# One core, a tuned layer kernel: the model axis of adaLN in three stretches instead of two, and half of the gate's work beside the output stage

## The chip, the cores and the metric

One core of one Trainium2 chip runs the kernel. The metric is the device time in microseconds, median of the runs shown. TensorE (PE) does the matmuls, VectorE (DVE) and ScalarE (ACT) the elementwise work, SyncE (SP) and ScalarE issue the transfers.

## The reference

One layer with adaLN: a normalised input, modulated by a shift and a scale, is projected; 8 differential attention heads (group A) and 8 retention heads (group B) use the projection; one output projection follows, and a gate.

```python
mod = silu(c) @ ada_w + ada_b                 # ada_w: 4096 x 12288
shift, scale, gate = split(mod, 3)
mod_c = silu(c_ctx) @ ada_w[:, :2*D] + ada_b[:2*D]
h  = rms_norm(x,   norm_w) * (1 + scale)   + shift     # 256 x 4096
hc = rms_norm(ctx, norm_w) * (1 + scale_c) + shift_c   # 256 x 4096
proj = h @ w_in                               # q, k, v and gate columns of 16 heads
pc   = hc @ w_in[:, k and v columns]
...                                           # attention, retention, per-head norm, silu
y = concat([o_d, o_r]) @ w_out                # 256 x 4096 @ 4096 x 4096
return x + gate * y
```

## The kernel before, in words

Every matmul of a projection is done three times in float32r: the weights are split into a high part `whi` (a cast on ScalarE, L390) and a rest `wlo` (a subtraction on VectorE, L391), and the activations into `hh` and `hl` (in the output stage `ohh` and `ohl`); L404 to L406 multiply high by high, high by rest, rest by high. The 4096 model rows are 32 k-tiles of 128. A **unit** is one load of two k-tiles of weights (`raw`, three buffers), two `whi` and two `wlo` (four buffers each, so two units' worth) and 24 matmuls for keys and values ("kv": four row tiles, latent and context) or 12 for queries and gate columns ("qg": two row tiles). A heads have 512 columns, B heads 384.

Since `h` needs adaLN's shift and scale of a k-tile before that k-tile can be multiplied, the work is staged:

- **Stage 1**: TensorE takes adaLN of k-tiles 0 to 19 (`pa` L264, then `pm` L280 for each chunk of 1 or 2 k-tiles), and between its steps the kv matmuls of heads A0 to A4 over the k-tiles that are ready (L555 to L557).
- **Stage 2**: the kv of the other 11 heads (`FIRST`: A5 to A7, B0 to B7) over k-tiles 0 to 19; the partial sums are stored to DRAM (`p_dram`). Beside them VectorE takes adaLN of k-tiles 20 to 31 in three chunks of 4 (`ada2_task`: 32 loads `ada2` of 512 KB and two multiply-adds `acc` for each, L327; at a chunk's end 32 small matmuls `pm` L335 on TensorE, and the modulation of the chunk's `h`).
- **Main loop**: for each head the kv over k-tiles 20 to 31 (partials loaded at L491, added at L499) and the qg over all 32; attention or retention of earlier heads, and the gate, run beside it, steps of them after each unit (`between`). The gate is 128 steps: a load `graw` of 512 KB and two multiply-adds `gacc` on VectorE (L937, the first L935), and after every 16 steps a small matmul and a store of one column block of 512. `gate_rate` steps follow each unit: 2 in kv units of A heads, 1 in those of B heads, 0 in qg units.
- **Output stage**: 8 column blocks of 512, 16 units of 12 matmuls each (`O0_0` to `O7_15`). When a block is done, its gate row `gt` and input `xr` are loaded and the result `ot` is formed on VectorE (L1045, L1046).

Gate loads, `gacc`, `acc`, partials, `gt`, `xr`, `ot` and `ostg` (a head's output on its way back from DRAM) share one pool `a4` of 9 buffers. The instructions of an engine run in the order that the scheduler has laid down, which follows the program's order but lets later ones pass one that waits for a buffer. One SP queue issues all loads of `raw`, `ada`, `graw` and of the partials, in its own order.

Of the kernel before, what the change touches and what calls it, by code (L numbers as in the profile page):

```python
# [10 lines left out]
F32 = mybir.dt.float32  # L11
# [7 lines left out]
P = 128  # L19
# [19 lines left out]
K1 = 20  # L39
CHUNKS = [1, 1] + [2] * 9  # L40
CHUNKS2 = [4, 4, 4]
LEAD = 0.3
NS = 5
ADAB = 6
# [37 lines left out]
def hybrid_kernel(es, tc, x, c, ctx, c_ctx, norm_w, ada_w, ada_b, w_in, q_norm_w, k_norm_w,  # L82
# [132 lines left out]
    c0s2 = [K1 + sum(CHUNKS2[:j]) for j in range(len(CHUNKS2) + 1)]  # L215
# [87 lines left out]
    def ada2_task():  # L303

        work = [(j, k) for j in range(len(CHUNKS2)) for k in range(KT)]
        ahead = []

        def load():
            if len(ahead) < len(work):
                j, k = work[len(ahead)]  # L310
                ahead.append(ada_load(c0s2[j], CHUNKS2[j], k, f"ada2_{j}_{k}")[0])

        for _ in range(ADAB - 1):
            load()
        yield
        for i, (j, k) in enumerate(work):
            w = ahead[i]
            cn = CHUNKS2[j]
            n = cn * P
            if k == 0:  # L320
                acc = [a4.tile([P, 2 * n], F32, name=f"acc{j}_{v}", tag="a4") for v in range(2)]
            for v in range(2):
                cv = cT[:, v, k:k + 1]
                if k == 0:
                    nc.vector.tensor_scalar(acc[v], w, cv, None, op0=ALU.mult)
                else:
                    nc.vector.scalar_tensor_tensor(acc[v], w, cv, acc[v], op0=ALU.mult, op1=ALU.add)  # L327
            load()
            if k == KT - 1:
                yield  # L330
                pm = aux_tile([P, cn, 4], f"pm2_{j}")
                for q in range(cn):
                    for s in range(2):
                        for v in range(2):
                            nc.tensor.matmul(pm[:, q, 2 * s + v:2 * s + v + 1],  # L335
                                             acc[v][:, s * n + q * P:s * n + (q + 1) * P], ones[:, 0:1],
                                             start=True, stop=True)
                modulate(c0s2[j], cn, pm)
            yield
# [141 lines left out]
    def head_units(hd, qg, ktseq, part=False, rest=False):  # L481
# [4 lines left out]
        bank = Bank(f"ps{hd.name}{'p' if part else ''}_{qg}", nrt)  # L486
# [118 lines left out]
    ada2 = ada2_task()  # L605
    next(ada2)
    n_units = len(FIRST) * K1 // 2
    n_steps = len(CHUNKS2) * (KT + 1)
    done = [0, 0]

    def between1(i):
        done[0] += 1
        while done[1] < n_steps and done[1] < done[0] / (n_units - 10) * n_steps:
            next(ada2, None)
            done[1] += 1

    for nm in FIRST:
        run_units(head_units(heads[nm], 0, pairs(0, K1), part=True), between1)
    for _ in ada2:
        pass  # L620
# [291 lines left out]
    gate_done = [False]  # L912

    def gate_task():
# [35 lines left out]
        gate_done[0] = True  # L950
# [18 lines left out]
    def gate_step():  # L969
        next(gate, None)  # L970
# [127 lines left out]
```

## Time and profile before

| what | value |
|---|---|
| time, median of 3 runs | 2552.03 us (2547.63 to 2555.55) |
| profiled execution | 2548.96 us, its span 2547.1 us |
| mean granted clock of TensorE | 0.993 |
| PE busy | 2496.5 us (98%) |
| DVE busy | 1718.8 us (67%) |
| ACT busy | 1000.9 us (39%) |
| stages: 1 / 2 / main loop A, B / output, us from the span's start | 50 to 442 / to 944 / 956 to 1648, to 2169 / to 2541 |

The span is what lies between the first and the last instruction. TensorE's busy time counts overlapping matmuls, so the pace is read from matmul starts: in the output stage one in 0.234 us at 512 columns, for B heads one in 0.174 us at 384 columns.

### The profile page before, as it was taken

How to read it: one execution, taken by the hardware profiler on the slowest of the kernel's cores; microseconds unless marked ns; L12 is line 12 of the kernel's file. 1: busy time of each engine (PE TensorE's matmuls, PEld its weight loads, DVE VectorE, ACT ScalarE, POOL GpSimd, SP SyncE). 2: the span in 40 equal slices, each digit the busy share in tenths (PEclk: the TensorE clock that was granted, in tenths of full speed). 3: DMA queues.
4: the chain of work that ended last, by engine and by line, in shares of the span. 5: the costliest groups of instructions: out<-in, count | busy, mean ns of one | idle time of the engine just before them, and what ended most of it. 6: DMA issues, size and time to landing. Idle time of an engine off the chain costs nothing.

```text
span 2547.1 us, 36352 instructions
## 1 busy us (share of the span) xinstructions
PE 2496.5 (98%) x12634; PEld 2125.9 (83%) x12634; DVE 1718.8 (67%) x3028; ACT 1000.9 (39%) x2011; POOL 46.3 (2%) x49
## 2 busy tenths in 40 slices
PE   7899999999999999999999999999999999999999
PEld 4566667888999997788888888899999999788887
DVE  5555556965979546777877887777777666655554
ACT  5222222222323233354445444544444445444443
POOL 0000000000000000000000000000000000000000
PEclk8999999999999999999999999999999999999999
DMA  9989887865777438766776677556666556666765
GB/s 317 300 277 299 279 284 260 292 213 162 246 239 234 143 110 273 235 217 198 240 228 213 203 243 230 178 184 196 199 206 204 165 157 193 195 220 208 225 211 175
DMA packets 495159, 563.70 MB, mean 221 GB/s; under 512 B 31664, under 2 KB 385264, under 8 KB 494976
## 3 DMA queue, kind: packets, MB, share of 16 engines
q1 hardware_dynamic: 478208, 526.54, 65.9%
q10 hardware_dynamic: 16768, 34.85, 4.0%
q8 instruction: 99, 1.62, 0.3%
q14 instruction: 84, 0.69, 0.1%
HBM read 538.17 MB, written 23.09 MB: 220 GB/s over the span
## 4 chain that ended last, share of the span: by engine, by line
PE 90%; DMA 6%; DVE 2%; SPq 1%; issue 1%; ACT 1%; DVEq 0%; POOL 0%; ACTq 0%; POOLq 0%
PE psA L405 8%; PE psA L406 8%; PE psA L404 8%; PE psB L405 6%; PE psB L406 6%; PE psB L404 6%; PE psO L404 5%; PE psO L405 5%; PE psO L406 5%; DMA ada<-in_ada_w_dram 3%; PE pa L264 3%; DMA graw<-in_ada_w_dram 1%; PE psA3s L555 1%; PE psA1s L555 1%; PE psP L556 1%; PE psP L555 1%
## 5 line engine op out<-in xcount | busy, mean ns | idle before, releaser
L390 ACT CAST whiB<-rawB 128x384 fp32r<-128x384 f32 x512 | 259.6, 512 | 471.0 <-PE psB L406 197.9
L390 ACT CAST whiA<-rawA 128x512 fp32r<-128x512 f32 x412 | 253.9, 620 | 425.0 <-PE psA L406 242.0
L391 DVE TENSOR_TENSOR wloB<-rawB,whiB 128x384 fp32r<-128x384 f32 x512 | 279.2, 553 | 173.3 <-ACT whiB L390 169.7
L391 DVE TENSOR_TENSOR wloA<-rawA,whiA 128x512 fp32r<-128x512 f32 x412 | 281.8, 687 | 152.3 <-ACT whiA L390 147.9
L405 PE MATMUL psA<-wloA,hh 128*128 128x512 f32 x896 | 357.6, 399 | 2.1 <-DVE wloA L391 2.1
L406 PE MATMUL psA<-whiA,hl 128*128 128x512 f32 x896 | 355.5, 397 | 0.0
L404 PE MATMUL psA<-whiA,hh 128*128 128x512 f32 x896 | 319.2, 398 | 0.0
L405 PE MATMUL psB<-wloB,hh 128*128 128x384 f32 x896 | 303.7, 339 | 2.2 <-DVE wloB L391 2.2
L406 PE MATMUL psB<-whiB,hl 128*128 128x384 f32 x896 | 302.4, 337 | 0.0
L391 DVE TENSOR_TENSOR wloO<-rawO,whiO 128x512 fp32r<-128x512 f32 x256 | 175.6, 691 | 157.2 <-ACT whiO L390 156.9
L404 PE MATMUL psB<-whiB,hh 128*128 128x384 f32 x896 | 263.9, 339 | 1.2 <-ACT whiB L390 1.2
L390 ACT CAST whiO<-rawO 128x512 fp32r<-128x512 f32 x256 | 158.0, 620 | 200.0 <-PE psO L406 164.0
L327 DVE SCALAR_TENSOR_TENSOR acc<-ada,cT,acc 128x1024 f32<-128x1024 f32 x186 | 233.8, 1277 | 0.0
L937 DVE SCALAR_TENSOR_TENSOR gacc<-graw,cT,gacc 128x512 f32<-128x512 f32 x248 | 184.7, 745 | 51.5 <-DMA graw<-in_ada_w_dram 49.7
L405 PEld LDWEIGHTS psA<-wloA,hh 128*128 128x128 f32 x896 | 168.7, 188 | 42.7 <-DVE wloA L391 4.1
L405 PE MATMUL psO<-wloO,ohh 128*128 128x512 f32 x512 | 203.9, 399 | 0.0
L406 PE MATMUL psO<-whiO,ohl 128*128 128x512 f32 x512 | 203.5, 398 | 0.0
L404 PEld LDWEIGHTS psA<-whiA,hh 128*128 128x128 f32 x896 | 168.5, 189 | 39.7
L406 PEld LDWEIGHTS psA<-whiA,hl 128*128 128x128 f32 x896 | 168.7, 188 | 39.0
L405 PEld LDWEIGHTS psB<-wloB,hh 128*128 128x128 f32 x896 | 169.0, 189 | 4.4 <-DVE wloB L391 3.7
L406 PEld LDWEIGHTS psB<-whiB,hl 128*128 128x128 f32 x896 | 168.9, 189 | 0.3
L404 PE MATMUL psO<-whiO,ohh 128*128 128x512 f32 x512 | 164.0, 399 | 3.9 <-ACT ohh L1015 3.9
(395 smaller groups left out, 4213.3 us busy)
## 6 DMA issues: line engine op xcount, KB each, us to landing
ada<-in_ada_w_dram SPq DMA_DIRECT2D x512, 256.0 KB, 4.8
rawA<-in_w_in_dram SPq DMA_DIRECT2D x412, 256.0 KB, 3.2
rawB<-in_w_in_dram SPq DMA_DIRECT2D x256, 256.0 KB, 3.2
graw<-in_ada_w_dram SPq DMA_DIRECT2D x128, 512.0 KB, 4.9
rawO<-in_w_out_dram SPq DMA_DIRECT2D x128, 512.0 KB, 4.4
rawB<-in_w_in_dram SPq DMA_DIRECT2D x256, 128.0 KB, 2.9
p_dramA<-kvqgA ACTq DMA_DIRECT2D x16, 512.0 KB, 5.1
kvqgA<-p_dramA SPq DMA_DIRECT2D x16, 512.0 KB, 7.6
```

The source lines that it names most:

```text
L264: m = nc.tensor.matmul(self.pa[32 * g:32 * (g + 1), :], cpad[:, 2 * kt:2 * kt + 32], tiles[k], start=(u0 == 0 and i < 4), stop=(u0 + nk == ...
L327: nc.vector.scalar_tensor_tensor(acc[v], w, cv, acc[v], op0=ALU.mult, op1=ALU.add)
L390: nc.scalar.copy(hi, raw[:, k])
L391: nc.vector.tensor_tensor(lo, raw[:, k], hi.bitcast(F32), op=ALU.subtract)
L404: nc.tensor.matmul(pt[:, :ncol], a, hi, start=f, stop=False)
L405: nc.tensor.matmul(pt[:, :ncol], a, lo, start=False, stop=False)
L406: nc.tensor.matmul(pt[:, :ncol], b, hi, start=False, stop=e)
L555: nc.tensor.matmul(pt, a, hi, start=f, stop=False)
L556: nc.tensor.matmul(pt, a, lo, start=False, stop=False)
L937: nc.vector.scalar_tensor_tensor(acc, raw[:, k], cT[:, 0, kt:kt + 1], acc, op0=ALU.mult, op1=ALU.add)
```

## The change

The model axis is cut into three stretches, k-tiles 0 to 13, 14 to 23 and 24 to 31. TensorE takes adaLN of the first alone (8 chunks: two of 1, six of 2 k-tiles). Stage 2 is now a loop over `LATER`: its first pass does the 11 heads over the first stretch (77 units) while VectorE takes adaLN of k-tiles 14 to 23 in chunks of 4, 4 and 2; its second pass does all 16 heads over the second stretch (80 units; partials are loaded, added to and stored again) while VectorE takes the last 8 k-tiles in chunks of 4 and 4. In the main loop the kv of each head is left with 4 units instead of 6, and the gate has one step after each kv unit for A and B heads alike, so 64 of its steps lie there. The rest are called after the units of the output stage (0.7 for each), and a block's output takes what steps its gate still lacks.

```diff
-K1 = 20
-CHUNKS = [1, 1] + [2] * 9
-CHUNKS2 = [4, 4, 4]
+K1 = 14
+CHUNKS = [1, 1] + [2] * 6
+LATER = [[4, 4, 2], [4, 4]]
...
+            for i, (c0, cn, k0) in enumerate(self.work):
...
+                for k, w in enumerate(self.ahead[i]):
+                    for v in range(2):
...
+                            nc.vector.scalar_tensor_tensor(acc[v], w, cv, acc[v], op0=ALU.mult, op1=ALU.add)
...
+                    pm = aux_tile([P, cn, 4], f"pm2_{c0}")
...
+    for lv, chunks in enumerate(LATER):
+        names = FIRST if lv == 0 else [f"A{h}" for h in range(8)] + [f"B{h}" for h in range(8)]
+        kts = pairs(*stretches[lv])
...
+            while done[1] < a2.n and done[1] < done[0] / (n_units - 10) * a2.n:
...
+            run_units(head_units(heads[nm], 0, kts, part=True, rest=lv > 0, tag=f"l{lv}"), between1)
...
-        gate_rate[0] = 0 if kind == "qg" else 2 if hd.kind == "A" else 1
+        gate_rate[0] = 0 if kind == "qg" else 1
...
-            run_units(head_units(hd, 0, pairs(K1, KT), rest=True), between)
+            run_units(head_units(hd, 0, pairs(*stretches[-1]), rest=True), between)
...
-    while not gate_done[0]:
-        gate_step()
...
     def out_after(nb, bank):
         def f():
+            while gate_at[1] <= nb:
+                gate_step()
...
     def between3(i):
+        while gate_at[0] < gate0 + i * 0.7 and gate_at[1] < NB:
+            gate_step()
```

**Place 1: VectorE in block 1 of the output stage.** `wloO1_10_1` is the rest of the second k-tile of unit 10 in block 1. Before, nothing but such subtractions stands here:

```order
L391 TENSOR_TENSOR wloO1_9_1_21683<-rawO1_9_21676,whiO1_9_1_21682 128x512
L391 TENSOR_TENSOR wloO1_10_0_21701<-rawO1_10_21698,whiO1_10_0_21700 128x512
L391 TENSOR_TENSOR wloO1_10_1_21705<-rawO1_10_21698,whiO1_10_1_21704 128x512
L391 TENSOR_TENSOR wloO1_11_0_21723<-rawO1_11_21720,whiO1_11_0_21722 128x512
L391 TENSOR_TENSOR wloO1_11_1_21727<-rawO1_11_21720,whiO1_11_1_21726 128x512
```

Now, between the same two subtractions:

```order
L948 SCALAR_TENSOR_TENSOR gacc4_20959<-graw4_10_21396,cT_108,gacc4_20959 128x512
L400 TENSOR_TENSOR wloO1_10_1_21631<-rawO1_10_21624,whiO1_10_1_21630 128x512
L948 SCALAR_TENSOR_TENSOR gacc4_20959<-graw4_11_21424,cT_108,gacc4_20959 128x512 x2
L948 SCALAR_TENSOR_TENSOR gacc4_20959<-graw4_12_21472,cT_108,gacc4_20959 128x512 x2
L948 SCALAR_TENSOR_TENSOR gacc4_20959<-graw4_13_21498,cT_108,gacc4_20959 128x512 x2
L948 SCALAR_TENSOR_TENSOR gacc4_20959<-graw4_14_21546,cT_108,gacc4_20959 128x512 x2
L948 SCALAR_TENSOR_TENSOR gacc4_20959<-graw4_15_21572,cT_108,gacc4_20959 128x512 x2
L946 TENSOR_SCALAR gacc5_21659<-graw5_0_21598,cT_108 128x512
L948 SCALAR_TENSOR_TENSOR gacc5_21659<-graw5_0_21598,cT_108,gacc5_21659 128x512
L721 TENSOR_TENSOR gal4_21648<-gacc4_20959,gah4_21647 128x512
L400 TENSOR_TENSOR wloO1_11_0_21665<-rawO1_11_21662,whiO1_11_0_21664 128x512
```

Gate steps of which the loads had to wait for buffers of `a4` stand here in one piece, and the next unit's `wlo` stands behind them. Counted over the output stage, the places where `gacc` stands densest on VectorE are these (units of a block, and what VectorE has to do from the first `wlo` of the first to the last instruction ahead of the next unit):

| block, units | `wlo` | `gacc` | `ot` | `gal` |
|---|---|---|---|---|
| 1, 9 and 10 | 4 | 14 | 4 | 1 |
| 2, 1 to 6 | 12 | 22 | 4 | 0 |
| 3, 1 to 7 | 14 | 22 | 4 | 1 |
| 4, 1 to 7 | 14 | 22 | 4 | 0 |
| 5, 1 to 4 | 8 | 15 | 4 | 0 |

**Place 2: the SP queue in block 2 of the output stage.** `rawO2_4` is the weights of unit 4. Before:

```order
L383 DMA rawO2_3_21909<-in_w_out_dram 128x2x512
L383 DMA rawO2_4_21931<-in_w_out_dram 128x2x512
L383 DMA rawO2_5_21953<-in_w_out_dram 128x2x512
L383 DMA rawO2_6_21975<-in_w_out_dram 128x2x512
L383 DMA rawO2_7_21997<-in_w_out_dram 128x2x512
```

Now, from `graw5_9` on, behind four more `graw` that follow `rawO2_3`:

```order
L929 DMA graw5_9_21945<-in_ada_w_dram 128x2x512
L929 DMA graw5_10_21993<-in_ada_w_dram 128x2x512
L392 DMA rawO2_4_21897<-in_w_out_dram 128x2x512
L929 DMA graw5_11_22019<-in_ada_w_dram 128x2x512
L392 DMA rawO2_5_21923<-in_w_out_dram 128x2x512
L929 DMA graw5_12_22067<-in_ada_w_dram 128x2x512
L392 DMA rawO2_6_21949<-in_w_out_dram 128x2x512
L929 DMA graw5_13_22093<-in_ada_w_dram 128x2x512
L929 DMA graw5_14_22119<-in_ada_w_dram 128x2x512
L929 DMA graw5_15_22167<-in_ada_w_dram 128x2x512
L929 DMA graw6_0_22193<-in_ada_w_dram 128x2x512
L392 DMA rawO2_7_21971<-in_w_out_dram 128x2x512
```

Between `rawO2_3` and `rawO2_7`, itself counted, the queue holds 16 loads of 512 KB where it held 4.

**Place 3: VectorE in stage 2, head B4.** `acc22` are the sums of the chunk of k-tiles 22 and 23, `md18` and `hm18` belong to the modulation of k-tiles 18 to 21. Before, in the same stage at head B3:

```order
L327 SCALAR_TENSOR_TENSOR acc2_0_6619<-ada2_2_6_6663,cT_108,acc2_0_6619 128x1024
L327 SCALAR_TENSOR_TENSOR acc2_1_6620<-ada2_2_6_6663,cT_108,acc2_1_6620 128x1024
L391 TENSOR_TENSOR wloB3_0_10_1_6465<-rawB3_0_10_6457,whiB3_0_10_1_6464 128x384
L327 SCALAR_TENSOR_TENSOR acc2_0_6619<-ada2_2_7_6703,cT_108,acc2_0_6619 128x1024
L391 TENSOR_TENSOR wloB3_0_12_0_6501<-rawB3_0_12_6497,whiB3_0_12_0_6500 128x384
```

Now:

```order
L400 TENSOR_TENSOR wloB4l0_0_2_1_5088<-rawB4l0_0_2_5080,whiB4l0_0_2_1_5087 128x384
L334 SCALAR_TENSOR_TENSOR acc22_0_4907<-ada2_22_6_4777,cT_108,acc22_0_4907 128x512
L334 SCALAR_TENSOR_TENSOR acc22_1_4908<-ada2_22_6_4777,cT_108,acc22_1_4908 128x512
L290 TENSOR_TENSOR md18_4837<-pm2_18_4820,modbias_109 128x16
L334 SCALAR_TENSOR_TENSOR acc22_0_4907<-ada2_22_6_4777,cT_108,acc22_0_4907 128x512
L334 SCALAR_TENSOR_TENSOR acc22_1_4908<-ada2_22_6_4777,cT_108,acc22_1_4908 128x512
L291 TENSOR_TENSOR md18_4837<-md18_4837,nwT_110 128x4x2
L334 SCALAR_TENSOR_TENSOR acc22_0_4907<-ada2_22_8_4817,cT_108,acc22_0_4907 128x512
L334 SCALAR_TENSOR_TENSOR acc22_1_4908<-ada2_22_8_4817,cT_108,acc22_1_4908 128x512
L301 SCALAR_TENSOR_TENSOR hm18_4840<-hm18_4840,md18_4837,rbc_175 128x256 x2
```

Over the whole of this stage 99 steps of adaLN now fall on 67 units, where 99 fell on 100 before.

## Rows read from the trace of the kernel before

**Rows 1.** The page, busy time of each engine over the span.

```profile
PE 2496.5 (98%) x12634; PEld 2125.9 (83%) x12634; DVE 1718.8 (67%) x3028; ACT 1000.9 (39%) x2011; POOL 46.3 (2%) x49
```

**Rows 2.** Windows by stage: PE, PEld, DVE, ACT, POOL busy, clock, DMA share, GB/s.

```profile
50.00:442.00 392.00, 373.30 (x1888) 254.47 (x1885) 218.74 (x386) 89.22 (x160) 0.00 (x0) 0.99 0.89 285
442.00:944.00 502.00, 502.00 (x2669) 468.87 (x2668) 372.74 (x478) 145.56 (x282) 0.00 (x0) 1.00 0.66 208
956.00:1648.00 692.00, 689.88 (x3115) 558.20 (x3115) 525.63 (x991) 316.75 (x695) 27.20 (x21) 1.00 0.70 223
2240.00:2541.00 301.00, 301.00 (x1286) 241.99 (x1285) 159.16 (x236) 130.81 (x212) 0.00 (x0) 1.00 0.67 211
```

**Rows 3.** The chain that ended last, TensorE in stage 1: start, us, what.

```profile
137.33 0.79 PE pm L280 x8
...
306.36 2.04 PE pa L264 x16
...
317.02 1.85 PE pa L264 x16
...
324.68 1.85 PE pa L264 x16
...
331.88 0.79 PE pm L280 x8
...
368.74 0.79 PE pm L280 x8
```

**Rows 4.** The chain, TensorE at a chunk's end in stage 2.

```profile
624.17 2.79 PE pm L335 x26
...
765.49 2.35 PE pm L335 x22
...
769.01 0.32 PE psB3p L406
...
772.11 0.17 PE psB3p L404
...
906.79 3.46 PE pm L335 x32
```

**Rows 5.** Groups of VectorE instructions: count, busy us, mean ns, idle before, releaser.

```profile
L391 DVE TENSOR_TENSOR wloB<-rawB,whiB 128x384 fp32r<-128x384 f32 x512 | 279.2, 553 | 173.3 <-ACT whiB L390 169.7
L391 DVE TENSOR_TENSOR wloO<-rawO,whiO 128x512 fp32r<-128x512 f32 x256 | 175.6, 691 | 157.2 <-ACT whiO L390 156.9
L327 DVE SCALAR_TENSOR_TENSOR acc<-ada,cT,acc 128x1024 f32<-128x1024 f32 x186 | 233.8, 1277 | 0.0
L937 DVE SCALAR_TENSOR_TENSOR gacc<-graw,cT,gacc 128x512 f32<-128x512 f32 x248 | 184.7, 745 | 51.5 <-DMA graw<-in_ada_w_dram 49.7
L499 DVE TENSOR_TENSOR kvqgA<-psA,kvqgA 128x512 f32<-128x512 f32 x32 | 20.6, 680 | 0.0
L1045 DVE TENSOR_TENSOR ot<-psO,gt 128x512 f32<-128x512 f32 x16 | 10.4, 683 | 4.7 <-PE psO L406 4.7
```

**Rows 6.** A window of stage 2, in B heads; columns as in the group of stages.

```profile
640.00:704.00 64.00, 64.00 (x371) 64.00 (x370) 62.04 (x82) 21.22 (x45) 0.00 (x0) 1.00 0.79 251
```

**Rows 7.** Transfers by what they load: count, KB each, median us to landing.

```profile
graw<-in_ada_w_dram SPq DMA_DIRECT2D x128, 512.0 KB, 4.9
rawO<-in_w_out_dram SPq DMA_DIRECT2D x128, 512.0 KB, 4.4
```

**Rows 8.** A window at the gate's start in the main loop.

```profile
976.00:992.00 16.00, 16.00 (x70) 12.88 (x69) 14.86 (x22) 3.61 (x7) 0.00 (x0) 1.00 1.07 369
```

**Rows 9.** Timeline of PE at the end of block 0: start, us, what, idle before.

```profile
2227.78 0.80 PE L404 MATMUL psO<-whiO,ohh 128*128 128x512 f32 x1 [3.93 <-ACT ohh L1015]
2228.37 0.63 PE L405 MATMUL psO<-wloO,ohh 128*128 128x512 f32 x1
2228.80 0.63 PE L404 MATMUL psO<-whiO,ohh 128*128 128x512 f32 x1
...
2232.94 0.40 PE L404 MATMUL psO<-whiO,ohh 128*128 128x512 f32 x1
```

More of the change, by code (lines that the diff above doesn't have):

```diff
@@ L214, in hybrid_kernel @@
     c0s = [sum(CHUNKS[:j]) for j in range(len(CHUNKS) + 1)]
-    c0s2 = [K1 + sum(CHUNKS2[:j]) for j in range(len(CHUNKS2) + 1)]
+    stretches = [(0, K1)]
+    for cs in LATER:
+        stretches.append((stretches[-1][1], stretches[-1][1] + sum(cs)))
     ada_units = []
@@ L301, in modulate @@
                                                op0=ALU.add, op1=ALU.subtract)
[L303 to L329, printed above, removed]
-                yield
[L331 to L339, printed above, removed]
@@ L479, in dst, with head_units @@
             return self.t[i][:, rt % 2, :]
-    def head_units(hd, qg, ktseq, part=False, rest=False):
+    def head_units(hd, qg, ktseq, part=False, rest=False, tag=""):
         segs = a_segs(hd.h) if hd.kind == "A" else b_segs(hd.h)
@@ L485, in head_units @@
         nrt = 2 if qg else 4
-        bank = Bank(f"ps{hd.name}{'p' if part else ''}_{qg}", nrt)
+        bank = Bank(f"ps{hd.name}{tag}_{qg}", nrt)
         def before():
@@ L495, in after @@
                 d = hd.dst(rt, qg)
-                if part:
+                if rest:
+                    nc.vector.tensor_tensor(d, bank.t[rt][:, :hd.ncol], d, op=ALU.add)
+                elif part:
                     nc.scalar.copy(d, bank.t[rt][:, :hd.ncol])
-                elif rest:
-                    nc.vector.tensor_tensor(d, bank.t[rt][:, :hd.ncol], d, op=ALU.add)
                 else:
@@ L506, in head_units @@
             last = i == len(ktseq) - 1
-            units.append(Unit(segs[qg], kt0, nk, bank, f"{hd.name}_{qg}_{kt0}", i == 0, last, nrt,
+            units.append(Unit(segs[qg], kt0, nk, bank, f"{hd.name}{tag}_{qg}_{kt0}", i == 0, last, nrt,
                               after=after if last else None,
@@ L603, in hybrid_kernel, with between1 @@
     store_part(sheads[-1])
[L605 to L620, printed above, removed]
+    for lv, chunks in enumerate(LATER):
+        names = FIRST if lv == 0 else [f"A{h}" for h in range(8)] + [f"B{h}" for h in range(8)]
+        kts = pairs(*stretches[lv])
+        a2 = Ada2(chunks, stretches[lv][1])
+        steps = a2.steps()
+        n_units = len(names) * len(kts)
+        done = [0, 0]
+        def between1(i):
+            done[0] += 1
+            while done[1] < a2.n and done[1] < done[0] / (n_units - 10) * a2.n:
+                next(steps, None)
+                done[1] += 1
+        for nm in names:
+            run_units(head_units(heads[nm], 0, kts, part=True, rest=lv > 0, tag=f"l{lv}"), between1)
+        for _ in steps:
+            pass
     ada_cm.__exit__(None, None, None)
@@ L969, in gate_step @@
     def gate_step():
+        gate_at[0] += 1
         next(gate, None)
```

39 lines of the change are left out of this document (37 added, 2 removed).

## Prediction, made before the changed kernel was run

> **What bounds the kernel now.** First the page's row of engines [rows 1]: PE is busy 98% of the span, VectorE 67%, ScalarE 39%. That PE waits nowhere for long is to be seen in the windows by stage [rows 2]: stage 2 is busy throughout, the A part of the main loop lacks 2 us, the output stage from 2240 us on nothing, with 1286 matmuls in 301 us, one in 0.234 us. So the kernel is faster only if matmuls go away or in stage 1, where the chain [rows 3] shows PE beside adaLN; and it is slower wherever the changed order leaves PE without weights. How much work PE has in hand decides the second. It needs `whi` and `wlo` of a k-tile; four of each exist, so PE can be at most four k-tiles ahead of VectorE: in the output stage 4 x 6 matmuls x 0.234 = 5.6 us, for a B head 4 x 12 x 0.174 = 8.4 us. Raw loads lie before that. VectorE runs its instructions in order: its groups [rows 5] show `gacc` idle 51.5 us, 49.7 of it for `graw`, and what stands behind such a wait waits too.
>
> **The change, part by part.** The sum is made against the profiled execution's 2548.96 us (span 2547.1, so 1.9 lie around it).
>
> *Stage 1: three chunks less.* Chunks of two k-tiles end with `pm` at 137.33 and 368.74 us, six periods apart [rows 3]: 38.6 us each. A chunk's own main matmuls are 5 heads x 2 k-tiles x 12 = 120, 28.1 us at 0.234, and these move to later passes at the same price. The rest, 10.5 us, is adaLN: in the rows of one chunk `pa` takes 2.04, 1.85 and 1.85 us three times over (a fourth group of 16 is split), about 7.8 in all, `pm` 0.79, and some 2 are waits. Three chunks: -31.4 us. If the waits and the transfers behind them only move elsewhere: -26.
>
> *PE work for VectorE's chunks.* At a chunk's end stand 32 small matmuls: 2.79 + 2.35 + 3.46 = 8.6 us for 80 of them in the chain [rows 4], 0.108 each. Before there are 3 x 32, now 4 x 32 + 16: 48 more, +5.2 us. After one of the three bursts main matmuls ran at 0.32 us instead of 0.17 for about 3.4 us (769.01 to 772.11): half the pace, as at the lower of the two clocks, some 1.5 us. For two more bursts +1 (0 to 3).
>
> *VectorE in the second and third pass.* Stage 2's steps are denser, 99 on 67 units. In B heads a unit then asks of VectorE 1.48 x 2 x 1.277 + 2 x 0.553 = 4.9 us [rows 5] and PE does its 24 matmuls in 4.18. Over the 22 units of a chunk of 4 that is 0.7 x 22 = 15.6 us too much; the lead takes up to 8.4 of it, and the order lets `acc` slide into the last 10 units, which have no steps of their own. A window of before had VectorE busy 62 of 64 us with no loss on PE [rows 6], so near-full is not yet a loss. Bounds 0 and 16; I take +7, the excess beyond the lead. The third pass has 66 steps on 70 units, 0.94 x 2.55 + 1.1 = 3.5 us for a B unit and 3.8 for an A unit (of 5.6): it fits. Its 64 more additions of partials (0.68 us for A [rows 5]) are hidden in that slack, as are 32 loads and 32 stores of partials; without cover the additions would cost some 40. PE begins a head with banks that are free, so the additions at a head's end are not waited for.
>
> *Main loop.* A unit of kv costs the same in whichever pass it stands. The gate is thinner there, which PE does not feel: +1 at most for other waits at its start.
>
> *Output stage.* Here 64 loads and some 128 `gacc` arrive that were beside the main loop. On average they fit: a unit is 2.81 us of PE, and VectorE would need 1.38 + 0.7 x 1.49 = 2.4. But the steps do not stand evenly: loads of the gate wait for buffers of the common pool, which `gt`, `xr` and `ot` take when a block ends, and then stand in bunches (place 1 and the table of the change). What a bunch costs: VectorE's work in it, less the PE time of its units, less the lead at its start (four k-tiles less the one being multiplied, 4.2 us). With `gacc` 0.745, `wlo` 0.691, `ot` 0.683 [rows 5]:
> block 1: 4 x 0.691 + 14 x 0.745 + 5 x 0.69 = 16.6 for 2 units, 5.6: 11.0 - 4.2 = 6.8 (one `gacc` is of the shorter kind: 6.5).
> Block 2: 8.3 + 16.4 + 2.7 = 27.4 for 6 units, 16.9: 6.3.
> Block 3: 9.7 + 16.4 + 3.4 = 29.5 for 7, 19.7: 5.6.
> Block 4: 28.8 for 7: 4.9.
> Block 5: 5.5 + 11.2 + 2.7 = 19.4 for 4, 11.2: 4.0.
> Together 27. Nothing gives it back, since outside the bunches PE already runs at its own pace.
> The loads bunch likewise (place 2): 16 of 512 KB between `rawO2_3` and `rawO2_7`. The fastest stretch of before moves 369 GB/s [rows 8]; at that a load is 1.42 us and the sixteen 22.7. PE has about five units (three raw, two split) and three more that come meanwhile: 22.4 us. So transfers at their best pace just keep up and land no earlier than VectorE wants them; at the share of 0.67 for 211 GB/s [rows 2], that is 315 when full, they take 26.6, about 4 us late in each of four bunches, partly the same wait.
> The rule that bears on this: the Trainium skill, "DMA: Bandwidth & Descriptors", section "Where 436 GB/s comes from", puts a core's HBM traffic at about 358 GB/s and the fabric at 435. By 358 the sixteen would take 23.4 us and be 1 us late, by 435 19.3 and be in time; the row of 369 lies between, and nearer the first.
> Last, after a wait the clock: when PE stood 3.93 us for `ohh`, its next matmuls started 0.43 us apart (2228.37, 2228.80) instead of 0.234, until 2232.9 [rows 9], about 2 us lost. Five stalls of that size would lose 10, but where VectorE limits, PE's slower pace is partly hidden in the wait. For late loads and clock together I take +6. Output stage: +33, bounds 18 (lead fuller than counted, all of clock and loads hidden) and 55 (every cost in full, transfers at 315 GB/s).
>
> The sum: -31.4 + 5.2 + 1 + 7 + 1 + 33 = +15.8, so 2564.8 on the profiled basis. The median of the runs is 3.1 higher than the profiled execution; I put the forecast between the two bases, **2566 us**. 0.3% is 7.7 us, about what a measurement of this kernel tells from no change.
>
> **The rivals.**
> *A. The bunches are absorbed, faster.* The gate's steps would cost nothing if VectorE were done with a bunch before PE's work in hand is used up. Then 33 becomes at most 5, the other terms stay: -31.4 + 14.2 + 5 = -12, and with stage 2 free as well -19: 2530 to 2540. For it: PE loses nothing in stage 2 of before at 62 of 64 us [rows 6]. Against it: in block 2 it would need `gacc` at (16.9 + 4.2 - 8.3 - 2.7) / 22 = 0.46 us where the row has 0.745. It decides from there.
> *B. Half of it, no change.* If PE enters each bunch with the full four k-tiles, VectorE's bunches cost 1.4 less each, 27 - 7 = 20 or 21 in all, late loads and clock nothing, and stage 2 costs nothing: -31.4 + 6 + 21 = -4, about 2545 to 2556.
> *C. Transfers bind, slower still.* At 315 GB/s the four bunches of loads are each 4 us late on top of VectorE's wait, and five stalls lose 2 us each to the clock: the output stage costs 50, in all 2580 to 2592. For it: `graw` and `rawO` take 4.9 and 4.4 us to land even in an easy queue [rows 7]. Against it: the same queue ran at 369 once [rows 8].
> *D. VectorE binds stage 2* over all its B heads of the chunk of 4: the 16 in full and its waits, 2572 to 2580.
> That the change does nothing isn't open: matmuls of stage 1 and the order's bunches are both there.
>
> **How the numbers follow.** The forecast's own region, 2557 to 2578, 0.50; A 0.15; B 0.18; C 0.11; D 0.06. The range leaves out A and the far part of C: 2541 to 2588. Faster by over 0.3% (below 2544): A and a sliver of B, 0.17. Within (2544 to 2560): the rest of B and the low end of the forecast, 0.21. Slower: 0.62.
>
> **What would show it.** Stage 1 right: `pm` of chunks still 38.6 us apart, its last some 116 us earlier. In B heads of stage 2, `wlo` as the releaser of PE for 7 us in sum. In the output stage PE idle in five places, in units 10 to 11 of block 1 and from units 3 on in blocks 2 to 5, 4 to 7 us each, released by VectorE's `wlo`, with VectorE busy with `gacc` ahead of it, and no idle in blocks 6 and 7. I am wrong if PE's idle time there is under 15 us, if the wait before `wlo` is ScalarE's cast for a late `rawO` (C), or if the gain of stage 1 is far from 31, because its transfers, 285 GB/s before [rows 2], wait elsewhere.

## The result, and the profile after

The changed kernel takes **2596.4 us** (median of 4 runs, 2592.92 to 2599.05) against 2552.84 for the kernel before: ratio 1.017, 95% interval 1.0152 to 1.0188, some 44 us slower. The direction was as forecast (2566), the size was not: 14 us were forecast, and the time lies outside the range of 2541 to 2588.

The page's row of engines of the changed kernel, beside [rows 1]:

```profile
PE 2501.9 (97%) x12466; PEld 2128.1 (82%) x12466; DVE 1833.6 (71%) x3170; ACT 989.7 (38%) x2008; POOL 52.2 (2%) x49
```

Its windows by stage (stage 1; the two passes; main loop, A heads, B heads; output stage), columns as in [rows 2]:

```profile
50.00:327.00 277.00, 263.34 (x1312) 179.54 (x1309) 154.75 (x272) 64.22 (x115) 0.00 (x0) 0.97 0.88 283
327.00:688.00 361.00, 361.00 (x1926) 337.82 (x1926) 300.11 (x404) 111.63 (x219) 0.00 (x0) 1.00 0.75 238
688.00:1089.00 401.00, 399.43 (x1988) 355.11 (x1987) 301.40 (x427) 99.49 (x181) 3.09 (x1) 1.00 0.75 250
1089.00:1686.00 597.00, 591.83 (x2668) 478.32 (x2667) 403.58 (x791) 285.58 (x636) 29.14 (x19) 1.00 0.59 183
1686.00:2159.00 473.00, 461.19 (x2721) 449.29 (x2720) 340.27 (x733) 227.43 (x507) 15.37 (x17) 1.00 0.63 193
2159.00:2586.00 427.00, 392.13 (x1626) 303.79 (x1624) 300.32 (x472) 168.12 (x289) 2.20 (x4) 0.96 0.79 262
```

PE is never idle in the first pass and 1.6 us in the second, where VectorE is busy 300 of 361 and 301 of 401 us. It is idle 12 us in the B heads and 35 in the output stage (4 in each before). In the output stage the granted clock is 0.96 and the engines of the transfers are at 0.79; over the same stage before they were at 0.99 and 0.66.

The first matmul of each stage in the trace gives the stages' lengths in us. "Moved work" is what a stage should take after by its units alone (24 matmuls of 0.234 or 0.174 us for each that it gave or took). Stage 2 before is counted up to its last matmul, which the trace has at 955.8 us; the 944 in the table of times is too early.

| stage | before | by moved work | after | difference | forecast |
|---|---|---|---|---|---|
| 1 | 442.2 | 357.9 | 327.1 | -30.8 | -31.4 |
| passes beside VectorE's adaLN | 513.8 | 754.7 | 762.4 | +7.7 | +13.2 |
| main loop, A heads | 692.1 | 602.2 | 596.8 | -5.4 | } +1 |
| main loop, B heads | 521.3 | 454.5 | 472.9 | +18.4 | } |
| output | 372.1 | 372.1 | 426.3 | +54.2 | +33 |

The sum is +44.1; the spans differ by 44.0. Some 7 us between the A and B rows (an estimate) are attention of A heads: 116 of its matmuls now run beside B heads, 64 did before. In blocks of 192 matmuls, the output stage after against 45.0 us for an undisturbed block: 56.4, 62.2, 58.0, 52.2, 54.5, 53.2, 45.0, 45.0; before 51.0, 51.4 and six of 45.0. Not all of the loss is idle time: 98 matmuls of this stage start 0.25 to 0.5 us after the one ahead of them instead of 0.234, which makes 14.1 us; before it was 15 and 2.3 us.

How PE is held in block 1: a stretch of VectorE's timeline after, with what it waited for in brackets.

```profile
2249.70 0.68 DVE L400 TENSOR_TENSOR wloO<-rawO,whiO 128x512 fp32r<-128x512 f32 x1
2250.30 3.89 DVE L948 SCALAR_TENSOR_TENSOR gacc<-graw,cT,gacc 128x512 f32<-128x512 f32 x5
2254.54 4.69 DVE L948 SCALAR_TENSOR_TENSOR gacc<-graw,cT,gacc 128x512 f32<-128x512 f32 x6 [0.35 <-DMA graw<-in_ada_w_dram]
2259.91 0.49 DVE L946 TENSOR_SCALAR gacc<-graw,cT 128x512 f32<-128x512 f32 x1 [0.67 <-DMA graw<-in_ada_w_dram]
2260.43 0.75 DVE L948 SCALAR_TENSOR_TENSOR gacc<-graw,cT,gacc 128x512 f32<-128x512 f32 x1
2261.10 0.68 DVE L721 TENSOR_TENSOR gal<-gacc,gah 128x512 fp32r<-128x512 f32 x1
2261.70 1.89 DVE L400 TENSOR_TENSOR wloO<-rawO,whiO 128x512 fp32r<-128x512 f32 x3
```

This is place 1 of the order: 11.4 us without a `wlo`. The wait of PE that it makes does not end with a `wlo`, though. From ScalarE's and PE's timelines:

```profile
2259.34 0.62 ACT L720 CAST gah<-gacc 128x512 fp32r<-128x512 f32 x1 [11.82 <-DVE gacc L948]
2260.01 0.63 PE L956 MATMUL pg<-gah,onesr 128*32 128x512 f32 x1 [7.56 <-ACT gah L720]
```

PE stands at the gate's own small matmul `pg`, which needs `gah`, ScalarE's cast of the finished `gacc`; ScalarE stands 11.82 us for it too, with the casts of the next weights behind. In block 2 the chain of the changed kernel names something else (pieces under 0.05 us left out):

```profile
2275.86 0.70 DVE wloO L400
...
2278.02 8.85 DMA graw<-in_ada_w_dram
2286.93 8.64 DMA rawO<-in_w_out_dram
2295.64 11.44 DMA rawO<-in_w_out_dram
2307.17 0.63 ACT whiO L399
2307.84 1.22 PE psO L413 x2
2309.07 0.43 PE psO L414
```

Two weight loads land after 8.6 and 11.4 us, where the median before was 4.4 [rows 7]; PE waits for the second through ScalarE's cast, and afterwards its matmuls start 0.43 us apart instead of 0.234, as in [rows 9]. The engines of the transfers were not slow there. The first window holds this bunch; the second, in the second pass, holds units of 24 matmuls:

```profile
2284.00:2300.00 16.00, 11.36 (x42) 8.16 (x41) 14.59 (x22) 4.47 (x8) 0.00 (x0) 0.89 1.05 394
693.00:739.00 46.00, 46.00 (x198) 36.98 (x197) 44.26 (x48) 10.59 (x17) 0.00 (x0) 1.00 1.03 372
```

So the weights were late at 394 GB/s, and at 372 GB/s PE lost nothing elsewhere. By the trace the queue holds them. The SP queue's waits for landings in the output stage (us in total, times, longest), first before (one row), then after:

```profile
SPq L383 <- DMA rawO<-in_w_out_dram: 9.6, 12, 1.6
SPq L392 <- DMA rawO<-in_w_out_dram: 26.8, 17, 4.5
SPq L929 <- DMA graw<-in_ada_w_dram: 20.2, 13, 3.4
SPq L392 <- DMA graw<-in_ada_w_dram: 13.4, 12, 2.3
```

In the trace the loads of the queues share eight semaphores. In this stage 32 of the 237 issues after start within 0.15 us of the landing of the last load with the same semaphore, none of those before. In the chain above, `graw` lands at 2286.87 and `rawO` is issued at 2286.93; that one lands at 2295.57 and the next goes out at 2295.64. So in a bunch eight loads are under way, most of them the gate's, and a weight load is not issued until one is down. Eight loads of 512 KB at 394 GB/s take 10.6 us (an estimate), about what the late ones took.

Of PE's waits in the output stage the releasers after are:

```profile
PE psO L413 <- ACT whiO L399: 21.2, 15, 4.4
PE pg L956 <- ACT gah L720: 7.6, 1, 7.6
PE psO L414 <- DVE wloO L400: 5.2, 6, 1.9
```

So the forecast (VectorE's pieces) and late `rawO`, of which rival C spoke, both have a part, and late `rawO` the larger. In B heads VectorE stood behind a gate load, as at 2119.78, and the next `wlo` with it:

```profile
2114.55 1.53 DVE L948 SCALAR_TENSOR_TENSOR gacc<-graw,cT,gacc 128x512 f32<-128x512 f32 x2
2119.78 0.75 DVE L948 SCALAR_TENSOR_TENSOR gacc<-graw,cT,gacc 128x512 f32<-128x512 f32 x1 [3.70 <-DMA graw<-in_ada_w_dram]
...
2120.51 0.55 DVE L400 TENSOR_TENSOR wloB<-rawB,whiB 128x384 fp32r<-128x384 f32 x1
```

The theories tested: **G/W**, a gate step costs wherever it stands beside units of 12 matmuls, in the main loop as in the output stage (rival A: the B heads lose by denser attention). For the output stage, **V**, VectorE's bunches, against **T**, bunches of loads; and **B**, that it is the bunch in either, against **D**, the mean demand.

### The profile page after: what moved, and what is told of

It reads as the page before. It is cut to its first block, busy times and chain, and to the rows that moved or that the text cites. A ratio compares the mean times of both kernels' runs of the same rounds, so it can differ in the third digit from the quotient of the medians.

```text
span 2591.1 us, 36284 instructions
## 1 busy us (share of the span) xinstructions
PE 2501.9 (97%) x12466; PEld 2128.1 (82%) x12466; DVE 1833.6 (71%) x3170; ACT 989.7 (38%) x2008; POOL 52.2 (2%) x49
## 4 chain that ended last, share of the span: by engine, by line
PE 76%; DMA 14%; DVE 6%; issue 1%; ACT 1%; SPq 1%; POOL 0%; ACTq 0%; DVEq 0%; POOLq 0%
PE psA L414 6%; PE psA L415 6%; PE psA L413 6%; DMA graw<-in_ada_w_dram 6%; PE psB L414 3%; PE psB L415 3%; PE psB L413 3%; PE psO L414 3%; PE psO L413 3%; PE psO L415 3%; DMA rawO<-in_w_out_dram 2%; DMA ada<-in_ada_w_dram 2%; PE pa L267 2%; DVE gacc L948 2%; DMA rawB<-in_w_in_dram 1%
## 5 line engine op out<-in xcount | busy, mean ns | idle before, releaser
L334 DVE SCALAR_TENSOR_TENSOR acc<-ada,cT,acc 128x1024 f32<-128x1024 f32 (+1 forms) x310 | 354.8, 1171 | 0.0
L414 PE MATMUL psA<-wloA,hh 128*128 128x512 f32 x768 | 307.6, 401 | 4.1 <-DVE wloA L400 4.1
L400 DVE TENSOR_TENSOR wloA<-rawA,whiA 128x512 fp32r<-128x512 f32 x320 | 218.5, 688 | 123.7 <-ACT whiA L399 122.5
L415 PE MATMUL psA<-whiA,hl 128*128 128x512 f32 x768 | 305.1, 397 | 0.0
L399 ACT CAST whiA<-rawA 128x512 fp32r<-128x512 f32 x320 | 197.0, 619 | 257.1 <-PE psA L415 208.5
L413 PE MATMUL psA<-whiA,hh 128*128 128x512 f32 x768 | 268.1, 399 | 0.1
L415 PE MATMUL psB<-whiB,hl 128*128 128x384 f32 x768 | 259.1, 337 | 0.0
L399 ACT CAST whiB<-rawB 128x384 fp32r<-128x384 f32 x320 | 158.0, 511 | 187.5 <-PE psB L415 105.3
L400 DVE TENSOR_TENSOR wloB<-rawB,whiB 128x384 fp32r<-128x384 f32 x320 | 173.4, 553 | 65.5 <-ACT whiB L399 64.2
L413 PE MATMUL psB<-whiB,hh 128*128 128x384 f32 x768 | 217.0, 339 | 1.8 <-ACT whiB L399 1.8
L413 PE MATMUL psO<-whiO,ohh 128*128 128x512 f32 x512 | 167.7, 408 | 21.8 <-ACT whiO L399 21.2
```

The costliest lines, as they stand in the source:

```text
L399: nc.scalar.copy(hi, raw[:, k])
L400: nc.vector.tensor_tensor(lo, raw[:, k], hi.bitcast(F32), op=ALU.subtract)
L413: nc.tensor.matmul(pt[:, :ncol], a, hi, start=f, stop=False)
L414: nc.tensor.matmul(pt[:, :ncol], a, lo, start=False, stop=False)
L415: nc.tensor.matmul(pt[:, :ncol], b, hi, start=False, stop=e)
```

## The experiments

Stage lengths in us by the first matmul, as above; each row is one profiled execution. The times of e1, e8, e11, e13 and e14 are medians of 4 to 10 runs, the others single runs, with the kernel before at 2548.7 to 2549.9 beside them.

| run | time | passes | A heads | B heads | output |
|---|---|---|---|---|---|
| after | 2596.4 | 762.4 | 596.8 | 472.9 | 426.3 |
| e1_gate_main | 2591.81 | 772.3 | 614.2 | 490.4 | 380.4 |
| e2_gate_a2_b0 | 2602.37 | 770.4 | 614.1 | 456.7 | 425.0 |
| e3_half_gacc | 2591.91 | 767.5 | 596.8 | 470.6 | 422.4 |
| e4_half_graw | 2571.98 | 766.5 | 597.0 | 473.4 | 399.8 |
| e5_before_gate_out | 2597.11 | 513.8 | 691.7 | 517.0 | 423.3 |
| e6_late_partials | 2567.62 | 759.4 | 594.9 | 459.6 | 419.3 |
| e7_both_half | 2570.73 | 768.9 | 597.5 | 473.9 | 395.0 |
| e8_gate_in_pass | 2543.13 | 772.1 | 600.6 | 464.4 | 377.6 |
| e9_paced_07 | 2656.76 | 760.5 | 597.7 | 469.7 | 494.3 |
| e10_paced_05 | 2639.69 | 760.6 | 597.3 | 472.8 | 467.5 |
| e11_late_paced | 2622.25 | 765.6 | 593.8 | 458.6 | 464.6 |
| e12_gate_own3 | 2574.47 | 763.5 | 596.6 | 473.0 | 405.5 |
| e13_late_own3 | 2552.9 | 764.8 | 593.2 | 459.9 | 393.1 |
| e14_pass_and_out | 2550.49 | 774.6 | 596.7 | 463.1 | 381.5 |

How much a row means can be read where an edit leaves a stage alone. In the changed kernel and e3, e4, e7, e9, e10 and e12 the A heads take 596.6 to 597.7 us and the B heads 469.7 to 473.9. The passes scatter more. The first pass has the same 404 instructions of VectorE in the same order in every run of the new stages, and takes 360.0 to 366.4 us with the granted clock, here in e6 and e1:

```profile
327.00:687.00 360.00, 360.00 (x1930) 336.85 (x1929) 300.31 (x405) 112.23 (x220) 0.00 (x0) 1.00 0.75 239
327.80:694.20 366.40, 366.40 (x1930) 343.25 (x1929) 301.61 (x406) 112.42 (x220) 0.00 (x0) 0.98 0.74 235
```

**e5_before_gate_out: the gate's half alone, on the kernel before.**

```diff
         for _ in range(gate_rate[0]):
-            gate_step()
+            if gate_at[0] < 64:
+                gate_step()
...
-    while not gate_done[0]:
-        gate_step()
...
+            while gate_at[1] <= nb:
+                gate_step()
...
+        while gate_at[0] < gate0 + i * 0.7 and gate_at[1] < NB:
+            gate_step()
```

> The kernel before with one part of the change alone: the gate stops after 64 steps in the main loop (at its old rate, so all in A heads), the other 64 are called after the output stage's units and where a block's output needs them. Theory W (a gate step is dear wherever it stands beside units of 12 matmuls, whose own weights already take a load of 512 KB per 2.8 us): the output stage grows by 45 to 58 from 372 us as in the changed kernel, B heads of the main loop stay or gain a little; time 2592 to 2605. Rival X (the new stages share in that loss, by another state of queues and buffers at its start): it grows by 30 or less, time 2580 or less.

2597.11 us, output stage 423.3, both as theory W said. So 51 of the 54 us are the gate's, without the new stages.

**e1_gate_main: all of the gate in the main loop.**

```diff
-        gate_rate[0] = 0 if kind == "qg" else 1
+        gate_rate[0] = 0 if kind == "qg" else 2
```

> The changed kernel, but two gate steps after every kv unit of the main loop, so that all 128 lie there and none in the output stage. The time after was 43.6 us above before; by the traces the output stage holds +54 of it, the B heads of the main loop +17, stage 1 -31, the passes beside VectorE's adaLN +8. If the output stage's loss is the gate's alone, that stage takes 372 us again and the kernel some 2542. Theory G (the main loop's loss in B heads is gacc waiting for its load with wlo behind it): with twice as many steps in B heads the loss there grows by 10 to 15, 2550 to 2558. Rival A (it is the attention work that now falls on fewer units): B heads stay as they are, 2538 to 2546.

2591.81 us (ratio 1.0166, 1.014 to 1.0192): the output stage falls to 380.4, and the main loop takes most of the gain back, 17.4 us in A heads and 17.5 in B heads, and the passes lengthen by 9.9, of which 4.8 are the first pass. The total is far above what either theory said, since both left the A heads out. The order shows why: of the 256 `gacc` before, 175 stand beside kv units of 24 matmuls and 81 beside qg units; here 172 stand beside qg units. In the changed kernel's main loop 38 stand beside kv units and 82 beside qg units (8 ahead of it), although the code calls every step after a kv unit: a head's partials are asked for four units before its kv ends, which is now its first unit, and they take the buffers of the common pool first. To stand beside qg units was not dear in every case: the 75 `gacc` that stood beside qg units of A heads before were all in the first five of a head's 16 units, and PE waited 2.1 us in these heads; here 83 are spread over all 16.

**e2_gate_a2_b0: the same 64 steps, none in B heads.**

```diff
-        gate_rate[0] = 0 if kind == "qg" else 1
+        gate_rate[0] = 0 if kind == "qg" or hd.kind == "B" else 2
```

> The changed kernel with the same 64 gate steps in the main loop, but two after each kv unit of A heads and none in B heads; the output stage is unchanged. Theory G: the stalls of 19 us in B heads (7.6 before) fall to 8 or less, time about 2582 to 2586. Rival A: they stay, 2592 to 2598.

B heads fall by 16.2 to 456.7, 2 above what their units ask: theory G, rival A is out. But A heads grow by 17.3, so the total is missed (2602.37): a step costs there too when it slides far into the qg units.

**e6_late_partials: the partials asked for later.**

```diff
-before=before if rest and i == max(0, len(ktseq) - 4) else None
+before=before if rest and i == max(0, len(ktseq) - 1) else None
```

> The changed kernel, but each head's partials in the main loop (and the third pass) are asked for one unit before its kv ends instead of four, so that they don't take the pool's buffers from the gate: by the order 103 of 128 gacc of the main loop then stand beside kv units of 24 matmuls, where 38 do in the changed kernel (82 stand beside qg units of 12). Theory W: B heads go from 473 to about 457 to 462 us, output stage unchanged, time 2578 to 2588. Rival L: the partials land too late (6 us against a unit of 4.2) and the additions hold PE at the end of each head, B heads stay at 470 or more and the third pass grows by 10 or more: 2595 to 2615.

2567.62 us, 10 below the range: with the steps back beside kv units (103 of 128) the B heads take 459.6 as theory W said, and rival L is out. The output stage, which was to stay, is 7.0 shorter; A heads and passes gain 1.9 and 3.0. The loss in B heads is thus the place of the gate's steps, moved by a pool's buffers.

**e3_half_gacc, e4_half_graw, e7_both_half: VectorE's work or the loads.** Each leaves out part of the last 64 gate steps: one gacc of two, half of the load, or both.

```diff
-            for k in range(2):
+            for k in range(2 if v < 64 else 1):     # e3 and e7
...
-            nc.sync.dma_start(raw, ada_w[u * 2 * P:(u + 1) * 2 * P, ...
+            nk = 2 if v < 64 else 1                  # e4 and e7; both gacc of e4 read raw[:, 0]
+            nc.sync.dma_start(raw[:, 0:nk], ada_w[u * 2 * P:(u * 2 + nk) * P, ...
```

> The changed kernel, leaving out one of the two gacc of each of the last 64 gate steps; all loads stay. Theory V (VectorE's bunches of gacc make the output stage's loss): in block 2 VectorE then has 19 us for 6 units of 16.9, inside the lead, so the loss of 54 falls to 10 or 15 and the time to 2552 to 2560. Rival T (the gate's loads bunch in the queue and rawO lands late): the loss stays above 40, time 2580 to 2596.

> The changed kernel with half of each of the last 64 gate loads left out (256 KB instead of 512); both gacc read the half that is there. Theory V: the bunches are as long as before on VectorE, the output stage loses 30 or more, time 2574 to 2596. Rival T: sixteen loads of a bunch become ten in bytes, 14 us, well inside the lead, the loss falls to 15 or less, time 2552 to 2562.

> The changed kernel with both halves left out: the last 64 gate steps load half (256 KB) and do one gacc of the two. Leaving out the gacc alone took 4 us off the output stage's 426, the half loads alone 26. Theory T+V (transfers first, VectorE behind them): both together take off more than the sum, output stage 372 to 388, time 2533 to 2552. Rival P (what remains is the small work of each gate block and the waits for gt, xr and the pool's buffers): output stage 395 or more, time 2560 to 2572.

With half the `gacc` the output stage takes 422.4: theory V would have had some 385, T 412 or more. With half the loads it takes 399.8, between the two (T at most 387, V at least 402). With both it takes 395.0, where T and V together asked for 388 at most: rival P's number. What remains in blocks 2 to 5 of that run is 12.8 us; the largest single wait there is again for a `rawO`, which landed after 9.4 us, so P's cause is not shown by its number. In the chain of the run with half the `gacc` the loads are as late as in the changed kernel:

```profile
2286.64 9.22 DMA graw<-in_ada_w_dram
2295.93 11.68 DMA rawO<-in_w_out_dram
2307.71 0.63 ACT whiO L399
```

By blocks the half loads take 55.3, 68.9, 47.0, 45.8, 46.5, 46.6: next to nothing is lost in blocks 2 to 5, and block 1 is worse than in the changed kernel, with a bunch of 19 `gacc` in one unit (14 before the edit). VectorE's timeline there:

```profile
2258.83 4.68 DVE L949 SCALAR_TENSOR_TENSOR gacc<-graw,cT,gacc 128x512 f32<-128x512 f32 x6
2264.44 0.49 DVE L947 TENSOR_SCALAR gacc<-graw,cT 128x512 f32<-128x512 f32 x1 [0.93 <-DMA graw<-in_ada_w_dram]
2264.84 7.50 DVE L949 SCALAR_TENSOR_TENSOR gacc<-graw,cT,gacc 128x512 f32<-128x512 f32 x11
2272.26 0.69 DVE L721 TENSOR_TENSOR gal<-gacc,gah 128x512 fp32r<-128x512 f32 x1
```

By matmul starts PE stood 13.6 us for it, at `pg` as above. This wait at `pg` goes with the piece of `gacc`: 2.8 us with 7 of them (both halves left out), 7.6 with 14, 13.4 with 19. So V holds for that wait, T in blocks 2 to 5. The issues that start with a landing are 45 with half the `gacc` and 10 with half the loads, where the changed kernel has 32. Block 1 as a whole is not V's alone: with half the `gacc` it still takes 61.3 us, since late weights hold PE there instead (waits of 5.2 and 2.9 us). The smaller loads also made the order space the steps (1 to 4 `gacc` a unit in blocks 2 to 5 instead of up to 8), which leaves open whether fewer bytes or the spacing helped. Even steps are the next edit.

**e9_paced_07, e10_paced_05, e11_late_paced: even steps, by the ring of the weights.**

```diff
+            if v > 64:
+                raw = wpool.tile([P, 2, 512], F32, name=f"graw{cb}_{u}", tag="raw", bufs=RAWB)
+            else:
-            raw = a4.tile([P, 2, 512], F32, name=f"graw{cb}_{u}", tag="a4")
+                raw = a4.tile([P, 2, 512], F32, name=f"graw{cb}_{u}", tag="a4")
...
-        while gate_at[0] < gate0 + i * 0.7 and gate_at[1] < NB:
+        while gate_at[0] < gate0 + i * 0.5 and gate_at[1] < NB:     # e10, e11
```

> The changed kernel, all work kept, but from its 66th on a gate load takes its buffer from the three of raw instead of the common pool. In the order the gate's steps of the output stage then stand evenly, two gacc behind two of three units, and one graw between two rawO, at the same mean of 0.7 per unit. Theory B (the loss of 54 us in the output stage is made by bunches: sixteen loads and twenty gacc in one piece, while units need evenly spaced weights): output stage 376 to 392 us, time 2546 to 2562. Rival D (the mean demand of some 320 GB/s over the first 90 units, or the shared ring, is too much): output stage 405 or more, time 2575 or more.

> As the run with even gate steps at 0.7, at 0.5 per unit: the same 64 steps over all eight blocks, mean demand about 280 GB/s. Theory B: output stage 374 to 386 us, like the run at 0.7 within 8 us, time 2544 to 2556. Rival D: better than at 0.7 by 15 us or more, since the demand is what costs.

> Two mends together on the changed kernel: partials asked for one unit before a head's kv ends (that alone gave 2567.6 us, with 459.6 for the B heads), and even gate steps at 0.5 per unit in the output stage. If they add up (theories W and B): stage 1 and the passes as in the changed kernel, B heads 460, output stage 374 to 386, time 2520 to 2538, faster than before by 10 or more. Rival D: output stage 400 or more, time 2548 or more.

All three are far worse: 2656.76, 2639.69 and 2622.25 us (ratio 1.0285, 1.0262 to 1.0308), output stages of 494, 468 and 465. By number this is D, which named the shared ring beside the demand, and the run at 0.5 is better than that at 0.7 by 17 us, as D said. But the runs don't decide between bunches and demand, since the edit takes buffers from the weights. With three in the ring and loads landing in 4 to 8 us, at 1.5 to 1.7 loads in 2.8 us, the ring itself seems too short, while the engines of the transfers have room, as a window of the run at 0.5 shows (share 0.80). A longer ring was not tried:

```profile
2400.00:2450.00 50.00, 43.42 (x169) 31.68 (x168) 30.81 (x48) 16.50 (x29) 0.00 (x0) 0.97 0.80 247
```

**e12_gate_own3: even steps, with buffers of the gate's own.**

```diff
+            if v >= 76:
+                raw = atB.tile([P, 2, 512], F32, name=f"graw{cb}_{u}", tag="f4", bufs=3)
+            else:
-            raw = a4.tile([P, 2, 512], F32, name=f"graw{cb}_{u}", tag="a4")
+                raw = a4.tile([P, 2, 512], F32, name=f"graw{cb}_{u}", tag="a4")
```

> The changed kernel, all work kept; from its 76th load on the gate has three buffers of its own (those of the retention's pool, free by then) and takes none from the common pool, and the three of raw stay the weights'. In the order its steps then follow each other evenly in blocks 2 to 5, one to four gacc behind a unit, one graw between rawO; only block 1, unit 10 keeps a piece of 15. Theory B (the bunches make the loss): what block 1 loses stays (some 10 us), blocks 2 to 5 lose next to nothing, output stage 384 to 396 us, time 2554 to 2567. Rival D (the queue and the engines can't bring 1.7 loads per unit in time however they are spaced): output stage 410 or more, time 2580 or more.

Same work, same bytes, same mean rate, output stage 405.5 us and time 2574.47, both between the two forecasts and a little nearer D. By blocks the picture is B's in part: 57.3, 65.0, 49.2, 46.5, 51.6, 46.2. Blocks 2 to 5 lose 13.5 us instead of 37.9; block 1 still has its piece of `gacc` and loses 9.9 us in one gap between matmuls, at `pg`. Of the issues that start with a landing, 3 are left of 32. A window that is mostly its block 3 has the engines full and PE nearly so:

```profile
2340.00:2386.00 46.00, 44.84 (x188) 34.64 (x187) 40.78 (x64) 17.13 (x30) 0.00 (x0) 1.00 1.00 359
```

359 GB/s cost PE 1.2 us of 46. The changed kernel lost 3.7 in the same window at 298:

```profile
2340.00:2386.00 46.00, 42.32 (x169) 32.04 (x168) 35.20 (x54) 17.21 (x29) 0.00 (x0) 0.96 0.86 298
```

So in blocks 2 to 5 two thirds of the loss are the bunches, and the mean demand has the rest at most. The gate's own buffers also leave more of the common pool to `gt`, `xr` and `ot`; this run does not part that from the spacing.

**e13_late_own3: at 0.5 steps per unit, partials late.** As the run before it, with `gate0 + i * 0.5` and the edit of e6_late_partials.

> As the run with three buffers of the gate's own, at 0.5 steps per unit over all eight blocks, and with the partials asked for one unit before a head's kv ends. Theories W and B together: B heads 460, output stage 380 to 395, time 2522 to 2540, faster than before. Rival D: at 0.5 the demand is lower but spread over the whole stage, output stage 400 or more, 2545 or more.

2552.9 us, ratio 1.0008 (0.9993 to 1.0023), no difference from before. B heads 459.9 and the output stage 393.1 lie in the ranges; the total missed its upper end by 13 and lies where rival D's did. The passes took 5 us more than in e6_late_partials, nearly all in the first pass, at a granted clock of 0.99 against 1.00. Some six us more lie behind the stage: the gate's last block now ends with the last matmul, and its row is stored and loaded and `xr` fetched before the result can be formed, so the last matmul of `psO` starts 12.5 us ahead of the span's end instead of 5.6. Of the output stage's loss blocks 0 and 1 keep 22 us (54.8 and 57.4 against 45.0), while blocks 2 to 7 lose 10.5 in all.

**e8_gate_in_pass and e14_pass_and_out: the gate where units are long.** The gate's functions are moved ahead of the passes; adaLN's steps of the last pass end 36 units before it does, and these units call gate steps (e8: one or two, e14: one), with the partials late and 0.3 steps per unit in the output stage (e14: from the three own buffers).

```diff
-while done[1] < a2.n and done[1] < done[0] / (n_units - 10) * a2.n:
+while done[1] < a2.n and done[1] < done[0] / (n_units - (10 if lv == 0 else 36)) * a2.n:
...
+            if lv == 1 and done[0] > n_units - 36:
+                for _ in range(1+done[0]%2):
+                    gate_step()
```

> The changed kernel's stages, with the gate moved to where units have 24 matmuls: adaLN's steps of the third pass are done in its first 44 units, its last 36 units take one or two gate steps each (54), the main loop one for each kv unit with the partials asked for late, and the few left 0.3 for each unit of the output stage. By the order 114 gacc then stand in the third pass, 94 beside kv units, 28 beside qg units and 20 in the output stage. Theory W: stage 1 -31, passes +10 to +15, main loop -8 to +2, output stage +2 to +8: 2522 to 2545. Rival: a gate step costs the 0.4 us that it costs in the output stage wherever it stands: 2560 or more.

> The run with the gate's steps in the third pass again, with fewer of them there (one for each of its last 36 units) and the 28 that are left in the output stage with three buffers of their own. The run before had 410.5 us in the third pass, 600.6 and 464.4 in the main loop, 377.6 in the output stage. Expected by theories W and B: 402 to 405, 596 to 600, 460 to 464, 380 to 386; time 2532 to 2545, about as before it.

e8 takes 2543.13 us, ratio 0.9977 (0.9964 to 0.999): 0.2% below the kernel before and at the upper end of the range given. By stages it fits less well: against the moved work the passes are at +17 (10 to 15 expected), the main loop at +8 (-8 to +2), the output stage at +6 (2 to 8). e14 takes 2550.49 (1.0001, 0.9982 to 1.0019), no difference from before and above its range of 2532 to 2545. Its last pass took 414.6 us, where 402 to 405 was expected, with fewer gate steps than e8 (410.5): PE waited there 5.7 us for `wlo` in B heads, 1.0 in e8, and the granted clock was 0.98 against 1.00. Why fewer steps gave longer waits is open.

## Why the prediction was wrong

- *Stage 1, -31.4:* right, -30.8. Chunks of the changed kernel still end 38.6 us apart: (253.45 - 176.15) / 2 by the chain.

```profile
176.15 0.79 PE pm L283 x8
...
253.45 0.79 PE pm L283 x8
```

- *The passes, +13.2:* measured +7.7. The `pm` at 5.2 account for most; VectorE's +7 was too much, at most 2.5 is left for it in this profile. The seven profiles with the same two passes have 760.5 to 768.9 us, mostly by the clock, so the figure is good to a few us. PE was not idle in the first pass (361.00 of 361.00), though VectorE's work asked for more than a unit of PE in B heads. That the lead and the sliding of `acc` took all of it is argued, not shown.
- *Main loop, "+1 at most", the first step that failed:* measured +13. "The gate is thinner there, which PE does not feel" took the steps to stand where the code calls them. By the order they stand beside qg units, and far into them, because the partials now take the pool's buffers at a head's first unit. Shown by the runs without gate steps in B heads (-16) and with late partials (-13).
- *Output stage, +33, the second:* measured +54. That the steps stand in bunches and that these cost PE was right, and in block 1 VectorE's piece set one wait of 7.6 us where 6.5 was worked out, though it ended with `gah` and `pg` and not with `wlo`. Blocks 2 to 5 were sized by VectorE's work at 20.8 us, with 6 for late loads and clock; they lose 37.9. The term that was mis-sized is the loads', put at about 4 us a bunch, "partly the same wait": the sixteen loads made single weights land after 8 to 11 us, and with half of VectorE's work gone the same blocks still lose 34.8. The step behind it is the cover. I had given PE eight units, 22.4 us, for the sixteen loads; in block 2 the bunch's first `graw` is issued at 2277.00 and PE stands from 2289.1, 12 us later, for a weight load that the queue held behind the gate's. The price of the loads was not what failed, since they ran at 394 GB/s, above the 369 that it used. The clock's share was too small as well: slower pace alone cost 11.8 us more than before, where the +6 held late loads and clock together. Block 0 lost 5.4 more than before, which no term held. One sign of being wrong that the prediction named is met: 21.2 us of PE's idle time end with ScalarE's cast, 5.2 with `wlo`.
- *Rivals:* C, given 0.11, was right in what PE waits for, but not in its condition of transfers at 315 GB/s, and its 2580 to 2592 is still too low. A's and B's case, that bunches cost little, and D's, that the passes cost 16 us, did not come. The 369 GB/s [rows 8] was not the fastest stretch: the window above has 394 for 16 us and that of the second pass 372 for 46 us, and before had 392 from 964 to 980 us. The Trainium skill, "DMA: Bandwidth & Descriptors", section "Where 436 GB/s comes from", puts the limit of a core's HBM traffic at about 358; these windows lie 4 to 10% above it, and the measurement decides. The changed kernel lost PE's time at 298 as well as at 394, and PE lost none at 372, so the ceiling alone was not what decided.
- *Open:* what blocks 0 and 1 lose beyond the one wait (16.2 us more than before, of which it is 7.6), what the remaining 13.5 us of evenly spaced steps are, and how much of blocks 2 to 5 the eight loads under way explain: no run changed that number alone.

## What to carry to other kernels

Work that is called beside an output stage runs where buffers let it, not where the code calls it: read the order, count what stands between two weights on each queue, and price a bunch by its loads as well as by its arithmetic. Here a background step was cheap beside or just behind units that do much with each load (24 matmuls) and dear when spread over those that do little (12), so moving the long units out of a loop also took away the place where its background was free. And a buffer pool shared by two kinds of work decides the order of both: asking for partials one unit instead of four before they were needed was worth some 25 to 29 us here (one run).

## What the runs showed of the hardware

- Where the gate's loads stood in a bunch, the next load was issued when an earlier one had landed, with eight under way: 32 such issues in the output stage after, none before. The weights' loads then landed after up to 11.4 us instead of 4.4.
- The transfers reached 394 GB/s for 16 us and 372 GB/s for 46 us, the latter with PE busy 46.00 of 46 us.
- With a ring of three buffers for each stream the engines ran at a share of 1.00 and 359 GB/s for 46 us with PE busy 97% of it. With one ring of three for both streams they stayed at 0.74 to 0.80; that the loads under way limit there is a reading of these windows, not a test.
- The same pass took 360.0 us at a granted clock of 1.00 and 366.4 at 0.98, with PE busy throughout in both.
